# A hybrid decoder trunk on one core: the recurrent branch's gate products as three passes of split operands

## The chip, the core and the metric

The kernel runs on one of the eight cores of a Trainium2 chip. A core has a matrix engine (TensorE, PE in the profile, with its weight loads as PEld), a vector engine (VectorE, DVE), an activation engine (ScalarE, ACT), a general one (GpSimd, POOL), a queue engine that issues most transfers here (SyncE, SP), a work memory (SBUF) and the memory that products accumulate in (PSUM). The engines run side by side, each takes its own instructions in the order written, and semaphores tie them together. The metric is the time of one execution on the device in microseconds (us); times compared are medians of several runs.

## What is computed

Two layers over 256 positions of 2048 channels, all in float32. Each layer normalizes x, projects it (`w_in`), and feeds three branches: a convolution module, a recurrent branch (Griffin's RG-LRU), and sparse attention. Each branch has an output product; the three are weighted by gates, added and projected (`w_o`). Then a squared-ReLU MLP of 8192 channels. The part that the change touches is the two gate products of the recurrent branch, in 6 blocks of 128 channels:

```python
def rg_lru(x, wa, ba, wx, bx, lam):
    b, s, d = x.shape
    xb = x.reshape(b, s, RNN_BLOCKS, RNN_BLOCK_W)
    r = jax.nn.sigmoid((jnp.einsum('bsnc,ncd->bsnd', xb, wa).reshape(b, s, d) + ba).astype(jnp.float32))
    i = jax.nn.sigmoid((jnp.einsum('bsnc,ncd->bsnd', xb, wx).reshape(b, s, d) + bx).astype(jnp.float32))
    log_a = -RG_C * jax.nn.softplus(-lam.astype(jnp.float32)) * r
    a = jnp.exp(log_a)
    gated_x = jnp.sqrt(-jnp.expm1(2.0 * log_a)) * (i * x.astype(jnp.float32))
    _, h = lax.associative_scan(_lin_combine, (a, gated_x), axis=1)
    return h.astype(x.dtype)
...
        r = causal_depthwise_conv(r_x, rnn_conv_w[l], rnn_conv_b[l])
        r = rg_lru(r, rglru_wa[l], rglru_ba[l], rglru_wx[l], rglru_bx[l], rglru_lambda[l])
        p_b = (r * jax.nn.gelu(r_gate)) @ w_rnn_out[l]
```

## The kernel before

**Big products.** All weights stream through SBUF once, as tiles of 128x1024 (`raw`; 768 or 512 wide for the branches' output weights), issued by SP, with four buffers (`wpool`). Each tile is split in two: ACT copies it to `wh`, in the float32r format, and DVE subtracts, `wl = raw - wh`. What is multiplied is split likewise by `split` (`xhl`, `ua`, `rb`, `oh`, `yhl`, `ah`: first half the rounded value, second half the remainder). `tile2` then multiplies 128x128 weights in two passes: `wh` against both halves side by side (512 columns of a PSUM bank `pu`), and `wl` against the first half (256 columns). `unit2` runs 16 such pairs (two weight tiles; 4 or 6 pairs for branch outputs) and makes one unit: 128 output channels by 256 positions. `wnext` keeps three weight tiles ahead. There are four `pu` banks. A unit's bank is emptied by an ACT copy `z<-pu` and a DVE addition `z<-pu,z` (in the MLP's down and the output projection by two DVE additions to x); then it is free for the fourth unit after.

**Side work.** The three branches' small steps are generators (`conv_task`, `rnn_task`, `attn_task`) in a list `side`. `pump`, called between units and weight tiles, advances them while the planner's clocks `clk` for DVE and ACT lie behind PE's; `mm`, `act` and `tt` add an assumed cost to these clocks. So the traced order mixes side steps into the units. After that a scheduler orders each engine's instructions by its own estimate of when they are ready; `keep` pins an instruction behind the one traced before it on its engine..

**The recurrent branch.** `rnn_task` goes through its 6 blocks ("heads" here) in each layer. For head m, GpSimd issues the transfer of the two gate weights (`ruw`, 128x256); DVE makes the short convolution (`rconv`, 4 steps); PE multiplies the two weights by it in float32, 256 columns each, into a side bank `pv`; ACT makes `tr`, `ti` and `t` from it (tanh, tanh, tanh) and an exponential; DVE, ACT (square root) and DVE again prepare the scan; the scan's result times the gate `gg` is split (`rb`) for the branch's output product. ACT changes its function table between some of these (ACT_TABLE_LOAD). It runs once in each layer beside the units of the gates `ga`, of the convolution's output (`pa`, operand `ua`) and of the compression for attention (`wh,cst`).

Lines of the helpers: L134 `tt`, L138 `stt`, L153 `act`, L157 `mm`; L331 the GpSimd addition `ssq` of the norms; L420 the transfer `ruw`.

Of the kernel before, what the change touches and what calls it, by code (L numbers as in the profile page):

```python
# [10 lines left out]
F32R = mybir.dt.float32r  # L11
BF16 = mybir.dt.bfloat16
AF = mybir.ActivationFunctionType
ALU = mybir.AluOpType
# [4 lines left out]
S = 256  # L19
# [74 lines left out]
def trunk(ctx: ExitStack, tc: tile.TileContext, a, out):  # L94
    nc = tc.nc
    V, A, G, T = nc.vector, nc.scalar, nc.gpsimd, nc.tensor
# [10 lines left out]
    keep = tc.keep_in_program_order  # L107
    clk = dict(pe=0.0, v=0.0, act=0.0)

    def hl(dt=F32, name="hl"):  # L110
        return hlp.tile([128, 2, S], dt, tag="hl", name=name)

    def tmp(name="t"):
        return tp.tile([128, S], F32, tag="t", name=name)
# [4 lines left out]
    def big_ps():  # L119
        return psu.tile([128, 512], F32, tag="u", name="pu")  # L120

    def side_ps():
        return pss.tile([128, 512], F32, tag="s", name="pv")

    def fsz(ap):
        n = 1
        for s in ap.shape[1:]:
            n *= s
        return n


    def tt(o, x, y, op):
        clk["v"] += 0.07 + fsz(o) / 960
        return V.tensor_tensor(o, x, y, op=op)  # L134

    def stt(o, x, s, y, op0, op1):
        clk["v"] += 0.07 + fsz(o) / 960
        return V.scalar_tensor_tensor(o, x, s, y, op0=op0, op1=op1)  # L138

    def ts(o, x, s1, s2, op0, op1=None):  # L140
        clk["v"] += 0.07 + fsz(o) / 1920
        if op1 is None:
            return V.tensor_scalar(o, x, s1, None, op0=op0)
        return V.tensor_scalar(o, x, s1, s2, op0=op0, op1=op1)

    def act(o, x, f, bias=None, scale=1.0, accum=None):
        clk["act"] += 0.2 + fsz(o) / 1200
        kw = {}
        if bias is not None:
            kw["bias"] = bias  # L150
        if accum is not None:
            kw["accum_out"] = accum
        return A.activation(o, x, f, scale=scale, **kw)  # L153

    def mm(o, l, r, start, stop, passes=1):
        clk["pe"] += (passes * max(64, fsz(r)) if passes > 1 else max(256, fsz(r))) / 2400 + 0.002
        return T.matmul(o, l, r, start=start, stop=stop)  # L157

    def f32(ap):
        return ap.bitcast(F32)  # L160
# [20 lines left out]

    stream, ready = [], []

    def wtiles():
        raw = wpool.tile([128, 1024], F32, tag="raw", name="raw")
# [20 lines left out]
    def split(dst, src, scale=None):  # L208

        if scale is None:  # L210
            act(dst[:, 0, :], src, AF.Copy)
            tt(dst[:, 1, :], src, f32(dst[:, 0, :]), ALU.subtract)
        else:
            act(dst[:, 0, :], src, AF.Copy, scale=scale)
            stt(dst[:, 1, :], src, scale, f32(dst[:, 0, :]), ALU.mult, ALU.subtract)

    def tile2(p, w, i, r, k, n, between=None):
        h, lo = (v[:, i * 128:(i + 1) * 128] for v in w)
        r1 = mm(p, h, r.rearrange("p a s -> p (a s)"), k == 0, False)
        if between:  # L220
            keep(r1)
            between()
        r2 = mm(p[:, :S], lo, r[:, 0, :], False, k == n - 1)
        if between:
            keep(r2)

    def unit2(p, rhs, between=None):

        k, n = 0, len(rhs)
        while k < n:  # L230
            if k:
                pump()
            w = wnext()
            for i in range(min(8, n - k)):
                tile2(p, w, i, rhs[k], k, n, (between or {}).get(k))
                k += 1
# [19 lines left out]
                stream += halves(a["wup"][l, q * KT + m] if k == "up" else a["wdn"][l, q, m])  # L256


    side = []

    def step():
        v0, a0 = clk["v"], clk["act"]
# [107 lines left out]
    def causal_conv(o, u, w, b, k):  # L370

        ts(o, u, w[:, k - 1:k], b, ALU.mult, ALU.add)
        yield
        for d in range(1, k):
            stt(o[:, d:], u[:, :S - d], w[:, k - 1 - d:k - d], o[:, d:], ALU.mult, ALU.add)
            yield
# [38 lines left out]
    def rnn_task(l, rx, gg, rb_out):  # L415
        rw = par[:, l, P_RW:P_RW + 24]
        for m in range(6):
            rc = tmp("rconv")
            ruw = tmp("ruw")
            keep(G.dma_start(ruw, a["rgw"][l, m]))  # L420
            yield from causal_conv(rc, rx[m], rw[:, 4 * m:4 * m + 4], par[:, l, P_RB + m:P_RB + m + 1], 4)
            p = side_ps()
            mm(p[:, :S], ruw[:, :128], rc, True, True, 4)
            mm(p[:, S:], ruw[:, 128:], rc, True, True, 4)
            tr, ti, t2 = tmp("tr"), tmp("ti"), tmp("t2")
            act(tr, p[:, :S], AF.Tanh, bias=hpar[:, l, 132 + m:133 + m], scale=0.5)
            act(ti, p[:, S:], AF.Tanh, bias=hpar[:, l, 138 + m:139 + m], scale=0.5)
            s2, s4 = sp2[:, l, m:m + 1], sp4[:, l, m:m + 1]

            act(t2, tr, AF.Tanh, bias=s2, scale=s2)  # L430
            act(tr, tr, AF.Exp, bias=s4, scale=s4)
            yield
            stt(t2, tr, 1.0, t2, ALU.add, ALU.mult)
            ts(tr, t2, -1.0, 1.0, ALU.mult, ALU.add)
            stt(t2, t2, 2.0, t2, ALU.subtract, ALU.mult)
            act(t2, t2, AF.Sqrt, scale=-0.25)
            yield
            stt(ti, ti, 1.0, rc, ALU.add, ALU.mult)
            tt(ti, ti, t2, ALU.mult)
            h = rc  # L440
            clk["v"] += 0.6
            V.tensor_tensor_scan(h, tr, ti, 0.0, op0=ALU.mult, op1=ALU.add)
            yield
            tt(h, h, gg[m], ALU.mult)
            r = hl(F32R, "rb_")
            split(r, h, 0.5)
            rb_out.append(r)
            yield
# [241 lines left out]
    for i in range(8):  # L690
        nc.sync.dma_start(x[:, 2 * i:2 * i + 2, :], a["xT"][:, 2 * i:2 * i + 2, :])  # L691
        xs += [scaled(k, gain[:, 0, k:k + 1]) for k in (2 * i, 2 * i + 1)]
        u, c = i % 2, i // 2
        if c % 2 == 0:
            wt[u] = wtiles()
        wpart(wt[u], first[u + 2 * (c // 2)], slice(c % 2 * 512, c % 2 * 512 + 512))
        if u:
            for v in range(2):
                for k in range(4 * c, 4 * c + 4):
                    tile2(early[v], wt[v][1:], k % 8, xs[k], k, KT)  # L700
# [6 lines left out]
    for l in range(L):  # L707

        rc, rb = None, None
# [22 lines left out]
        def evict(nm, m, z):  # L732
# [16 lines left out]
            elif nm == "rgate":  # L749
# [5 lines left out]
                if m == 5:  # L755
                    rt = rnn_task(l, rx, gg, rbt)
                    side.append(rt)
# [26 lines left out]
        for ui, (nm, m) in enumerate(PLAN):  # L784
# [7 lines left out]
            if l == 0 and ui < 2:  # L792
                p = early[ui]
            else:
                p = big_ps()
# [22 lines left out]
        for m in range(KT):  # L818
            p = big_ps()
# [214 lines left out]
```

## Time and profile before

| | |
|---|---|
| median of 3 runs | 2848.22 us (2845.17 to 2848.49) |
| profiled execution, its time | 2845.14 us |
| its span in the trace | 2843.4 us |
| PE busy | 2831.4 us (100%), 16420 passes |
| DVE busy | 2094.7 us (74%) |
| ACT busy | 1473.0 us (52%) |
| GpSimd busy | 96.3 us (3%) |
| granted TensorE clock, mean | 0.999 |
| weight transfers (queue 1) | 529 MB, 56% of the DMA engines' time |

The span is what lies between the first and the last instruction of the trace; the execution's own time is 1.7 us longer. Busy time of an engine is a sum over stages. PE's busy time also covers passes that overlap (a pass of 512 columns is recorded with 0.39 us, and the next starts 0.23 us after it), so the distance between starts is a pass's price, and the recorded duration is not. On ACT and DVE an instruction may start about 0.1 us before the one ahead of it ends.

### The profile page before, as it was taken

What the parts mean: (1) busy time and instruction counts of PE and PEld (TensorE: products, weight loads), DVE (VectorE), ACT (ScalarE), POOL (GpSimd) and SP (SyncE); (2) the same over time, 40 slices, a digit from 0 to 9 for tenths busy, and PEclk for the clock granted to TensorE, in tenths of its full rate; (3) what the DMA queues carried; (4) which work ended last, traced back from release to release, by engine and by line L of the source; (5) the groups of instructions that cost most, each with busy time, mean ns of one, the idle gap of its engine ahead of it and who ended that gap; (6) DMA issues with size and microseconds to landing.
All of it is one profiled execution on the core that took longest, in us unless ns stands there. A gap on an engine that the chain in (4) does not pass through costs nothing.

```text
span 2843.4 us, 43117 instructions
## 1 busy us (share of the span) xinstructions
PE 2831.4 (100%) x16420; PEld 2489.8 (88%) x16420; DVE 2094.7 (74%) x3388; ACT 1473.0 (52%) x2253; POOL 96.3 (3%) x100
## 2 busy tenths in 40 slices
PE   9999999999999999999999999999999999999998
PEld 7888888888888888888888888888888888888887
DVE  7988888777676676666779888786777766756655
ACT  6547766555444343444544587565554444434444
POOL 0000000002000000000200000000020000000001
PEclk9999999999999999999999999999999999999999
DMA  7555654555555555555555556555555555555554
GB/s 241 191 188 177 216 179 161 170 193 192 185 192 189 190 191 188 192 190 189 192 186 192 185 187 215 160 165 178 195 186 192 190 189 192 188 190 191 190 191 148
DMA packets 153454, 534.28 MB, mean 188 GB/s; under 512 B 17312, under 2 KB 18208, under 8 KB 153248
## 3 DMA queue, kind: packets, MB, share of 16 engines
q1 hardware_dynamic: 152192, 529.15, 56.3%
q8 instruction: 128, 2.10, 0.3%
q0 software_dynamic: 768, 2.13, 0.3%
q14 instruction: 78, 0.64, 0.1%
q10 hardware_dynamic: 288, 0.26, 0.0%
HBM read 529.37 MB, written 2.10 MB: 187 GB/s over the span
## 4 chain that ended last, share of the span: by engine, by line
PE 99%; DMA 0%; DVE 0%; ACT 0%; issue 0%; SPq 0%; POOLq 0%; DVEq 0%; ACTq 0%
PE pu L157 96%; PE pv L157 3%; DMA raw<-in_win_dram 0%; PE pv L661 0%; DVE fin L134 0%; ACT wh L153 0%; PE pv L618 0%; DVE wl L134 0%; PE pv L527 0%; DVE xhl L138 0%; SPq L691 0%; POOLq L1026 0%; DVE sq L134 0%; DVEq L1026 0%; ACT sq L153 0%
## 5 line engine op out<-in xcount | busy, mean ns | idle before, releaser
L153 ACT ACTIVATE wh<-raw 128x1024 fp32r<-128x1024 f32 (+2 forms) x1036 | 1067.7, 1031 | 1288.2 <-PE pu L157 682.4
L157 PE MATMUL pu<-xhl,wh 128*128 128x512 f32 x4800 | 1677.1, 393 | 1.3 <-DVE xhl L138 0.8
L134 DVE TENSOR_TENSOR wl<-raw,wh 128x1024 fp32r<-128x1024 f32 (+2 forms) x1036 | 1228.9, 1186 | 593.8 <-ACT wh L153 573.0
L157 PE MATMUL pu<-xhl,wl 128*128 128x256 f32 x4800 | 1345.7, 281 | 0.4 <-DVE wl L134 0.4
L157 PEld LDWEIGHTS pu<-xhl,wh 128*128 128x128 f32 x4800 | 898.0, 187 | 199.0 <-ACT wh L153 1.5
L157 PEld LDWEIGHTS pu<-xhl,wl 128*128 128x128 f32 x4800 | 906.7, 189 | 3.5 <-DVE wl L134 1.2
L157 PE MATMUL pu<-ah,wh 128*128 128x512 f32 x2016 | 699.1, 391 | 0.0
L157 PE MATMUL pu<-ah,wl 128*128 128x256 f32 x2016 | 564.5, 280 | 0.0
L157 PEld LDWEIGHTS pu<-ah,wh 128*128 128x128 f32 x2016 | 377.0, 187 | 82.7
L157 PEld LDWEIGHTS pu<-ah,wl 128*128 128x128 f32 x2016 | 381.0, 189 | 0.0
L134 DVE TENSOR_TENSOR x<-x,pu 128x256 f32<-128x256 f32 x316 | 132.7, 420 | 87.9 <-PE pu L157 82.6
L157 PE MATMUL pu<-yhl,wh 128*128 128x512 f32 x512 | 177.5, 393 | 0.0
L157 PE MATMUL pu<-yhl,wl 128*128 128x256 f32 x512 | 141.7, 277 | 0.0
L331 POOL TENSOR_TENSOR ssq<-ssq,sq 128x256 f32<-128x256 f32 x55 | 74.1, 1347 | 1829.2 <-ACT sq L153 1829.2
L157 PEld LDWEIGHTS pu<-yhl,wh 128*128 128x128 f32 x512 | 95.8, 187 | 22.0
L134 DVE TENSOR_TENSOR z<-pu,z 128x256 f32<-128x256 f32 x268 | 111.4, 417 | 0.8 <-ACT z L153 0.8
L138 DVE SCALAR_TENSOR_TENSOR cacc<-u,hpar,cacc 128x255 f32<-128x255 f32 (+14 forms) x240 | 103.4, 462 | 0.0
L153 ACT ACTIVATE z<-pu 128x256 f32<-128x256 f32 x268 | 97.9, 366 | 1.1 <-PE pu L157 1.1
L157 PEld LDWEIGHTS pu<-yhl,wl 128*128 128x128 f32 x512 | 96.2, 188 | 0.2
L157 PE MATMUL pu<-oh,wh 128*128 128x512 f32 x192 | 67.4, 391 | 0.0
L134 DVE TENSOR_TENSOR z<-z,rb 128x256 f32<-128x256 f32 x136 | 57.4, 424 | 4.3
L138 DVE SCALAR_TENSOR_TENSOR s<-z 128x256 f32<-128x256 f32 x128 | 54.1, 424 | 4.3
(298 smaller groups left out, 1705.3 us busy)
## 6 DMA issues: line engine op xcount, KB each, us to landing
raw<-in_win_dram SPq DMA_DIRECT2D x340, 512.0 KB, 3.2
raw<-in_wup_dram SPq DMA_DIRECT2D x256, 512.0 KB, 4.2
raw<-in_wdn_dram SPq DMA_DIRECT2D x256, 512.0 KB, 4.3
raw<-in_wo_dram SPq DMA_DIRECT2D x64, 512.0 KB, 3.7
raw<-in_wro_dram SPq DMA_DIRECT2D x32, 384.0 KB, 3.1
raw<-in_wao_dram SPq DMA_DIRECT2D x32, 384.0 KB, 3.1
raw<-in_wco_dram SPq DMA_DIRECT2D x32, 256.0 KB, 3.3
raw<-in_cw_dram SPq DMA_DIRECT2D x16, 512.0 KB, 4.6
```

Source lines behind the costliest of these rows:

```text
L134: return V.tensor_tensor(o, x, y, op=op)
L138: return V.scalar_tensor_tensor(o, x, s, y, op0=op0, op1=op1)
L153: return A.activation(o, x, f, scale=scale, **kw)
L157: return T.matmul(o, l, r, start=start, stop=stop)
L331: G.tensor_tensor(ssq[0], ssq[0], q, op=ALU.add)
```

## The change

In `rnn_task`, the convolution's result and the gate weights are split in two, as all big operands are: ACT copies each to float32r (`rs`, `rws`), and GpSimd, not DVE, subtracts to make the remainders. The two float32 products of a head become six float32r passes of 256 columns: high by high, high by remainder, remainder by high, for each gate. A `yield` after the split lets other work be traced in between. In `tile2`, both passes of a pair are now pinned in program order whenever no side work is pending (before: only where a norm's steps are put between two passes).

```diff
@@ tile2
-        if between:
+        if between or not side:
             keep(r1)
+        if between:
             between()
         r2 = mm(p[:, :S], lo, r[:, 0, :], False, k == n - 1)
-        if between:
+        if between or not side:
             keep(r2)
@@ rnn_task
             yield from causal_conv(rc, rx[m], rw[:, 4 * m:4 * m + 4], par[:, l, P_RB + m:P_RB + m + 1], 4)
+            rs, rws = hl(F32R, "rs"), hl(F32R, "rws")
+            for dst, src in ((rws, ruw), (rs, rc)):
+                act(dst[:, 0, :], src, AF.Copy)
+                G.tensor_tensor(dst[:, 1, :], src, f32(dst[:, 0, :]), op=ALU.subtract)
+            yield
             p = side_ps()
-            mm(p[:, :S], ruw[:, :128], rc, True, True, 4)
-            mm(p[:, S:], ruw[:, 128:], rc, True, True, 4)
+            for i in range(2):
+                o, (wh, wl) = p[:, i * S:(i + 1) * S], (rws[:, k, i * 128:(i + 1) * 128] for k in range(2))
+                mm(o, wh, rs[:, 0, :], True, False)
+                mm(o, wh, rs[:, 1, :], False, False)
+                mm(o, wl, rs[:, 0, :], False, True)
```

The scheduler makes new orders of all this. Three places, as built. On ACT, fourth head of layer 1; before the change (here `rb` is the split of the head before, `tr<-pv` the first reader of the gate products, `z<-pu` the emptying of a unit's bank, `t_...` the head's tanh):

```order
L153 ACTIVATE wh<-raw 128x512
L153 ACTIVATE z<-pu 128x256
L153 ACTIVATE rb__16692<-rconv 128x256
L153 ACTIVATE gate<-gate 128x256
L153 ACTIVATE tr<-pv,hpar 128x256
L153 ACTIVATE ti<-pv,hpar 128x256
L153 ACTIVATE wh<-raw 128x1024
```

and the same head after it:

```order
L153 ACTIVATE wh<-raw 128x1024 x2
L153 ACTIVATE rb__16782<-rconv 128x256
L153 ACTIVATE rws<-ruw 128x256
L153 ACTIVATE rs<-rconv 128x256
L153 ACT_TABLE_LOAD
L153 ACTIVATE tr<-pv,hpar 128x256
L153 ACTIVATE ti<-pv,hpar 128x256
L153 ACTIVATE t_16880<-tr,sp_97 128x256
L153 ACTIVATE z<-pu 128x256 x4
```

Before, one bank is emptied ahead of `rb` and `tr`; after, two weight copies, `rb` and the two new copies stand in a row, and four banks are emptied behind `tr`, `ti` and `t`.

On PE at the same head, before:

```order
L157 MATMUL pu<-xhl,wh 128x512
L157 MATMUL pu<-xhl,wl 128x256
L157 MATMUL pv<-rconv,ruw 128x256 x2
L157 MATMUL pu<-xhl,wh 128x512
L157 MATMUL pu<-xhl,wl 128x256
```

and after:

```order
L157 MATMUL pu<-xhl,wh 128x512
L157 MATMUL pu<-xhl,wl 128x256
L157 MATMUL pv<-rs,rws 128x256 x6
L157 MATMUL pu<-ua,wh 128x512
L157 MATMUL pu<-ua,wl 128x256
```

The six passes stand together, at the end of a unit of `xhl`; the unit behind them is one of `ua`, in another bank.

On DVE, the first weight tiles after the two units with which the kernel starts (- before, + after):

```order
 L138 SCALAR_TENSOR_TENSOR xhl<-x,gain,xhl 128x256 x2
 L134 TENSOR_TENSOR wl<-raw,wh 128x512
-L134 TENSOR_TENSOR wl<-raw,wh 128x1024
-L134 TENSOR_TENSOR z<-pu,z 128x256 x2
+L134 TENSOR_TENSOR z<-pu,z 128x256
+L134 TENSOR_TENSOR wl<-raw,wh 128x1024
+L134 TENSOR_TENSOR z<-pu,z 128x256
 L134 TENSOR_TENSOR wl<-raw,wh 128x1024 x4
```

The emptying of the first unit's bank has moved ahead of the first weight tile of the third unit.

## Rows read from the trace of the kernel before

**Rows 1.** The page's part 1: busy us, share of the span, instructions

```profile
PE 2831.4 (100%) x16420; PEld 2489.8 (88%) x16420; DVE 2094.7 (74%) x3388; ACT 1473.0 (52%) x2253; POOL 96.3 (3%) x100
```

**Rows 2.** The page's part 4: the chain that ended last, by engine

```profile
PE 99%; DMA 0%; DVE 0%; ACT 0%; issue 0%; SPq 0%; POOLq 0%; DVEq 0%; ACTq 0%
```

**Rows 3.** PE's waits: engine, line <- releaser: us in total, times, longest

```profile
PE pv L157 <- POOL rc L905: 2.1, 1, 2.1
...
PE pv L157 <- DVE sq L134: 0.7, 1, 0.7
```

**Rows 4.** Stretches with the recurrent branch: from:to us, length, each engine's busy time

```profile
200.00:345.00 145.00, 145.00 (x842) 126.15 (x841) 121.30 (x225) 108.83 (x182) 5.72 (x10) 1.00 0.60 196
...
1600.00:1745.00 145.00, 145.00 (x846) 126.54 (x845) 120.25 (x222) 107.87 (x179) 5.50 (x10) 1.00 0.57 191
```

**Rows 5.** PE in time, fourth head of layer 1: start us, us, operation

```profile
1672.63 0.39 PE L157 MATMUL pu<-xhl,wh 128*128 128x512 f32 x1
1672.86 0.28 PE L157 MATMUL pu<-xhl,wl 128*128 128x256 f32 x1
1672.97 1.03 PE L157 MATMUL pv<-rconv,ruw 128*128 128x256 f32 x4
1673.65 0.58 PE L157 MATMUL pu<-xhl,wh 128*128 128x512 f32 x1
```

**Rows 6.** PE in time at the compression's split passes of 256 columns

```profile
301.13 0.28 PE L157 MATMUL pv<-wl,cst 128*68 128x256 f32 x1
301.25 0.28 PE L157 MATMUL pv<-wh,cst 128*68 128x256 f32 x1
```

**Rows 7.** Groups on ACT: operation and shapes, count | busy us, mean ns | idle before

```profile
L153 ACT ACTIVATE wh<-raw 128x1024 fp32r<-128x1024 f32 x932 | 989.0, 1061 | 1229.6 <-PE pu L157 661.3 <-issue 496.1 <-ACT xhl L153 45.8
...
L153 ACT ACTIVATE z<-pu 128x256 f32<-128x256 f32 x268 | 97.9, 366 | 1.1 <-PE pu L157 1.1
...
L153 ACT ACT_TABLE_LOAD x25 | 32.1, 1283 | 1.2 <-PEq L1020 0.7
...
L153 ACT ACTIVATE t<-tr,sp 128x256 f32<-128x256 f32 x12 | 7.2, 597 | 0.0
```

**Rows 8.** ACT in time, fourth head of layer 1

```profile
1672.72 0.36 ACT L153 ACTIVATE z<-pu 128x256 f32<-128x256 f32 x1
1673.16 0.42 ACT L153 ACTIVATE rb__16692<-rconv 128x256 fp32r<-128x256 f32 x1
...
1675.09 0.46 ACT L153 ACTIVATE tr<-pv,hpar 128x256 f32<-128x256 f32 x1
1675.45 0.47 ACT L153 ACTIVATE ti<-pv,hpar 128x256 f32<-128x256 f32 x1
```

**Rows 9.** A group on DVE: the addition that empties a bank

```profile
L134 DVE TENSOR_TENSOR z<-pu,z 128x256 f32<-128x256 f32 x268 | 111.4, 417 | 0.8 <-ACT z L153 0.8
```

**Rows 10.** GpSimd's additions (ns min/median/max), one of them and DVE around it

```profile
L331 POOL TENSOR_TENSOR ssq<-ssq,sq x55: 925/1372/1466, 637.8 to 2824.1; 128x256 f32<-128x256 f32 x55
...
637.77 1.47 POOL L331 TENSOR_TENSOR ssq<-ssq,sq 128x256 f32<-128x256 f32 x1 [132.36 <-ACT sq L153]
...
636.25 0.47 DVE L138 SCALAR_TENSOR_TENSOR xhl<-x,gain,xhl 128x256 fp32r<-128x256 f32 x1
637.42 1.23 DVE L134 TENSOR_TENSOR wl<-raw,wh 128x1024 fp32r<-128x1024 f32 x1 [0.69 <-ACT wh L153]
638.56 0.96 DVE L138 SCALAR_TENSOR_TENSOR xhl<-x,gain,xhl 128x256 fp32r<-128x256 f32 x1
```

**Rows 11.** PE in time at the start, at 20 us and after the sums of squares

```profile
1.46 4.44 PE L683 MATMUL pv<-wz 128*128 128x512 bf16 x12 [1.46 <-DVE wz L680]
...
20.31 0.39 PE L157 MATMUL pu<-xhl,wl 128*128 128x256 f32 x1 [0.16 <-DVE wl L134]
...
41.39 0.37 PE L157 MATMUL pu<-xhl,wl 128*128 128x256 f32 x1
```

**Rows 12.** Stretches at the end; behind POOL's busy time stands the granted clock

```profile
2836.00:2837.00 1.00, 0.15 (x1) 0.16 (x2) 0.38 (x2) 0.18 (x1) 0.61 (x1) 1.00 0.70 246
...
2838.00:2839.00 1.00, 0.00 (x0) 0.00 (x0) 1.00 (x3) 0.00 (x0) 0.00 (x0) 0.50 0.45 156
```

More of the change, by code (lines that the diff above doesn't have):

```diff
@@ L180, in trunk @@
     G.memset(ebase, 2.718281828459045)
-    stream, ready = [], []
+    stream, ready, side = [], [], []
     def wtiles():
@@ L219, in tile2 @@
         r1 = mm(p, h, r.rearrange("p a s -> p (a s)"), k == 0, False)
+        if between or not side:
+            keep(r1)
         if between:
-            keep(r1)
             between()
         r2 = mm(p[:, :S], lo, r[:, 0, :], False, k == n - 1)
-        if between:
+        if between or not side:
             keep(r2)
@@ L256, in trunk @@
                 stream += halves(a["wup"][l, q * KT + m] if k == "up" else a["wdn"][l, q, m])
-    side = []
     def step():
```

## The prediction

> **What bounds the kernel now.** I read the page from the top: the busy table, the chain, then what PE waited for, then the stretches in which the recurrent branch runs, and there single instructions. PE is busy for 2831.4 of 2843.4 us [rows 1], and the chain that ended last is PE for 99% of the span [rows 2]. After the first 8 us, PE's only waits that the profile lists are 0.7 us for the sums of squares at 40 us and 2.1 us at the very end [rows 3], and 0.16 at 20 us [rows 11]. So nothing can be gained by feeding PE better; time goes down by taking passes off PE, and goes up by whatever makes PE wait. The reader should next see how little room stands behind that full PE: in the two stretches of 145 us where the recurrent branch runs, DVE is busy for about 120 us and ACT for 108 us, and PE for all 145 [rows 4]. DVE and ACT take their work strictly in the order written, so in these stretches an instruction that comes late holds up everything behind it, the weight splits and the emptying of the `pu` banks too.
>
> **The change on PE: passes.** A head's two gate products stand today as four records, 0.68 us from the first to the next weight pass, and that pass is 0.19 us longer than usual (0.58 against 0.39): 0.87 us [rows 5]. A split pass of 256 columns that is not the last of a run starts 0.12 us after the one before [rows 6]; six are 0.70 us. That is 0.17 us a head, 12 heads: **-2.0 us**. It lies on the bound engine, so it is a gain in full. Four more waiting instructions on PE cost some 0.09 us each, as the weight pass at 41.39 does, 0.37 us long instead of 0.28 [rows 11]: +0.3.
>
> **The change on ACT, GpSimd and DVE.** A head gets two ACT copies of 0.4 us and two GpSimd subtractions in a row (24 copies, 24 subtractions in all). ACT has the time as a sum. But the products no longer start when the short convolution and the small weight have arrived: they start after ACT has copied both and GpSimd has made both remainders. GpSimd's price is read from the `ssq` additions of the same size: 0.93 to 1.47 us [rows 10]. Of that about 0.6 is work: the one at 637.77 ends at 639.24, 0.59 after the DVE subtraction that ran when it began (637.42 + 1.23). And DVE pays as well: the `xhl` step that takes 0.47 us alone takes 0.96 us beside GpSimd [rows 10]. The bounds for a remainder are thus 0.6 and 1.5 us; I take 0.9, the nearest row being the one with the least DVE work beside it. The Trainium skill, "SBUF — State Buffer", section "Who interferes with whom", says that a DVE instruction with two SBUF inputs and a GpSimd instruction that reads SBUF lock each other out, and whichever comes first keeps the shared port to its end. The trace agrees (0.59 us after, 0.96 for 0.47). By that rule alone, each subtraction costs DVE up to 0.49 us, 24 x 0.49 = 11.8 us if all of it fell on the path; by the trace most of it falls beside a full PE and costs nothing by itself.
>
> **What the new order does with it.** The end is set by where those late products stand in the fixed orders. I laid the changed order out with the trace's durations: every engine takes its rows in order; each starts when the row before it is done and what it reads or overwrites is free, 0.04 us after the releaser; a remainder takes 0.9 us, or ends 0.6 after the DVE subtraction in its way. Done on the kernel before, this puts no wait over 0.1 us on PE between 45 us and the last product, as the trace shows, and its end is 0.15% off the trace. Done on the changed order, PE waits at a dozen places. The fourth head of layer 1 shows all kinds, and can be followed by hand. *Copies:* on ACT now stand wh, wh, rb, rws, rs in a row, and the second wh needs the buffer that PE's last pass ahead of the six reads. So when PE reaches the six, 1.06 us of wh and three copies of 0.41 are still to come; followers on ACT start about 0.10 before the end of the one ahead (0.36 between tr and ti, both 0.46 to 0.47 long) [rows 7, 8]: 1.06 + 3 x 0.41 - 0.3, with the hand-offs **2.1 us** of waiting. *Remainders:* the weight's begins 0.3 us before the last copy ends and meets a DVE subtraction (1.23 us long [rows 10]), 1.2 us; then 0.9 for the other; less the 0.3 and the first pass: **1.6 us**. *Banks:* the unit right behind the six needs a `pu` bank, and on ACT four z<-pu stand behind tr, ti and t. After the sixth pass (0.28): 0.36 + 0.36 + 0.50 + 0.36 on ACT and 0.42 of z on DVE [rows 7 to 9], with the hand-offs: **2.3 us**. Together 6.0 us at one head. Before, z<-pu (1672.72) runs 2.4 us ahead of tr there, so the bank is free long before PE asks for it [rows 8].
>
> The other places, found in the same way, in us of PE waiting. Layer 0: third head 1.2 (remainder) and 2.4 (bank); fourth 0.4 (remainder), then 1.0 and 1.2 for wh and wl that stand behind the copies; 2.0 near 415 us, a bank behind attention's small steps, whose order moved too; 0.4 at the first pass of the output projection. Layer 1: third head 2.8 (the table load of 1.28 us stands between the six and tr), fourth 6.0, fifth 1.6 (wl) and 1.2 (bank), then 0.9 and 0.9, and again 0.4. That is 8.6 + 13.8 = 22.4 us, and each wait costs 0.09 more, as above: +1.2.
>
> *Start.* With the order pinned, z moves ahead of wl on DVE at 19 us: the subtraction starts 0.4 later, ACT's next step too, and PE, which waits 0.16 us there now [rows 11], waits for 1.1; with the sums of squares some 0.7 later: +1.9, between 0 and 2.4. Elsewhere pinning turns nothing but a few pairs around, which costs nothing on PE.
>
> **The sum**, on the profiled execution's own 2845.1 us: -2.0 + 0.3 + 22.4 + 1.2 + 1.9 = +23.8, 2868.9. That execution lies 3.1 us below the median of the three runs (2848.2, from 2845.2 to 2848.5); half of that added, I say **2870 us**. With remainders of 0.6 us the same layout gives 1 us less, with 1.5 us 3 more; so the size of GpSimd's step is not what decides, but its place in the orders.
>
> **The rivals.** *The remainders are ready in time* (not slower). DVE, ACT and GpSimd run ahead of PE enough, as they do now, and only the passes change: 2845.1 - 2.0 + 0.3, up to 2845 with a start that costs 2: 2843 to 2846, at most 0.2% under the median. It decides where a head's copies and remainders end before PE reaches its six passes. For it: today nothing of these stretches holds PE, though DVE and ACT are busy for three quarters of them and more [rows 4]. Against: at the fourth head the copies, whose price is known, come 2.1 us late by themselves. 0.08. *Only part of the waits.* The copies and remainders hold PE, but z and wl have more lead than I give them: 5 to 8 us of waits, 2849 to 2853: 0.08. *The clock falls too.* Near the end PE has a wait of 2 us and little to do after it, and the granted clock is 0.50 in the stretch that begins at 2838, the 1.2 GHz level, while it is 1.00 up to 2837 [rows 12]. Three waits within 7 us at one head are much the same. What it takes to come back is seen at the start, 12 passes in 4.44 us instead of 12 x 0.23 [rows 11]: 1.7 us for each fall. Two to six falls, and the DVE time of the lock with them: 2874 to 2890. The Trainium skill, "TensorE: Matmul & The Clock Gate", section "Part 1", has the array fall to half rate when PE idles and return with activity; the trace agrees (0.50 after the idle end), and that page speaks against waits that follow each other. 0.20. The change not doing what it says isn't a rival: the passes stand in the order as written.
>
> **Chances.** Forecast as laid out, 2856 to 2877: 0.64. Clock as well: 0.20. Part of the waits 0.08, in time 0.08. Faster by over 0.2% (the least that a measurement of this kernel tells from none) would need 2842.5: 0.03. Within 0.2%, up to 2853.9: 0.12. Slower 0.85. The range reaches from 2850, which leaves out the in-time rival, to 2886.
>
> **What would show it.** In the profile after: PE's waits at 230 to 345 us and 1640 to 1770 us, put down to POOL rs, ACT rs, DVE z and wl, about 20 us in all; six passes of 0.12 at each head; `rs` and `rws` subtractions of 0.9 to 1.4 us; the MLP stretches unchanged to 0.1%. I am wrong in the main step if PE waits under 8 us in these stretches; wrong on the start if PE's waits before 45 us are as now; the clock rival shows as a granted clock under 1 in a window around a head.

## The result, and the profile after

The changed kernel takes **2880.61 us** (median, 2878.96 to 2881.62), the kernel before 2847.14 (2845.17 to 2848.49): ratio **1.0123**, 95% interval 1.0111 to 1.0135. It is 33.5 us slower. The forecast was 2870, slower, with a range of 2850 to 2886: the sign and the range hold, the likeliest case was 10.6 us too low. Two of the four runs of the kernel before lie at 2845 to 2846 us and two at 2848; beside the experiments below its median is 2845.0 to 2845.3. The profiled execution of the changed kernel has a span of 2878.3 us, 34.9 more than the one of before.

Parts 1 and 4 of its page (busy time by engine, the chain that ended last), which answer to [rows 1] and [rows 2]:

```profile
PE 2846.1 (99%) x16444; PEld 2498.0 (87%) x16444; DVE 2103.9 (73%) x3388; ACT 1482.4 (52%) x2277; POOL 120.5 (4%) x124
...
PE 96%; issue 2%; DVE 1%; ACT 1%; DMA 1%; POOL 0%; SPq 0%; POOLq 0%; DVEq 0%; ACTq 0%
```

PE's idle time is 2878.3 - 2846.1 = 32.2 us, where it was 12.0: 20.2 us of the 34.9 are waits. The other 14.7 are in PE's busy time, although its passes became cheaper. A wait counts for more from start to start than as idle time, because the pass ahead of it is recorded longer than its price; counted so, as the prediction did, the waits come to 23.7 us (the table and the start, below). What is left of the second part is where the prediction fell short.

What PE waited for (engine, line <- releaser: us in total, times, longest), the view of [rows 3]:

```profile
PE pu L157 <- DVE z L134: 11.6, 6, 2.8
PE pv L157 <- POOL rs L426: 2.5, 2, 1.4
...
PE pv L157 <- DVE wl L134: 2.0, 2, 1.1
PE pv L157 <- ACT rs L153: 2.0, 1, 2.0
PE pu L157 <- DVE wl L134: 1.9, 5, 0.8
...
PE pv L157 <- DVE sq L134: 1.4, 1, 1.4
```

`DVE z`, the banks, has 11.6 us, more than half of the 20.2 that came with the change. GpSimd, the engine that the change gives new work, releases PE late twice, for 2.5 us in all. 24 subtractions took this long (ns min/median/max):

```profile
L426 POOL TENSOR_TENSOR rs<-rconv,rs x12: 732/917/1822, 237.4 to 1747.6; 128x256 fp32r<-128x256 f32 x12
...
L426 POOL TENSOR_TENSOR rws<-ruw,rws x12: 727/885/2229, 235.2 to 1746.7; 128x256 fp32r<-128x256 f32 x12
```

The stretches of [rows 4], an undisturbed one, and four short ones (from:to us, length, busy time of PE, PEld, DVE, ACT, POOL, then the granted clock):

```profile
200.00:345.00 145.00, 140.04 (x811) 122.77 (x810) 119.12 (x213) 106.21 (x183) 19.66 (x22) 0.98 0.55 183
...
720.00:1420.00 700.00, 700.00 (x4041) 617.08 (x4040) 469.61 (x648) 315.02 (x409) 17.25 (x13) 1.00 0.57 190
...
1600.00:1745.00 145.00, 134.03 (x760) 116.77 (x759) 110.76 (x195) 94.54 (x155) 12.33 (x17) 0.96 0.51 167
...
272.00:280.00 8.00, 6.89 (x24) 5.92 (x24) 5.78 (x15) 4.99 (x11) 0.00 (x0) 0.57 0.26 96
419.00:423.00 4.00, 4.00 (x15) 3.39 (x16) 3.92 (x15) 0.69 (x2) 0.42 (x1) 0.57 0.18 69
1695.00:1700.00 5.00, 4.51 (x17) 3.88 (x18) 4.30 (x11) 3.08 (x7) 0.00 (x0) 0.66 0.43 152
1709.00:1717.00 8.00, 5.94 (x21) 5.10 (x22) 6.50 (x17) 6.37 (x14) 0.00 (x0) 0.57 0.07 22
```

The recurrent stretches lose PE time and have a clock below 1; the MLP (720 to 1420) is as before. The last four rows find the low clock: a mean of 0.57 over 8 us, at the levels 0.5 and 1, is 6.9 us at the lower one (1.2 GHz). Together 6.9 + 3.4 + 3.4 + 6.9 = 20.6 us; each spell begins inside or right behind a PE wait of 1.7 us or more. What that costs is seen where the clock comes back, at 422.5 us (PE in time):

```profile
420.83 0.63 PE L157 MATMUL pu<-rb__2968,wh 128*128 128x512 f32 x1
421.26 0.41 PE L157 MATMUL pu<-rb__2968,wl 128*128 128x256 f32 x1
421.47 0.63 PE L157 MATMUL pu<-rb__3345,wh 128*128 128x512 f32 x1
...
422.64 0.39 PE L157 MATMUL pu<-xhl,wh 128*128 128x512 f32 x1
422.88 0.28 PE L157 MATMUL pu<-xhl,wl 128*128 128x256 f32 x1
422.99 0.40 PE L157 MATMUL pu<-xhl,wh 128*128 128x512 f32 x1
```

A pair takes 421.47 - 420.83 = 0.64 us at the low level and 0.35 at the full one. So each us at the low level in which PE works loses 0.46 us: up to 9.4 us for 20.6. PE is idle in some 2.5 us of that time, so I put it at 8 to 9.

Now the place that the prediction did by hand, the fourth head of layer 1. PE, ACT, GpSimd and one step of DVE in time (start, us, engine, line, operation, in brackets the idle time before and what ended it); for before see [rows 5] and [rows 8]:

```profile
1703.96 0.27 PE L157 MATMUL pu<-xhl,wl 128*128 128x256 f32 x1
1706.18 0.38 PE L157 MATMUL pv<-rs,rws 128*128 128x256 f32 x1 [1.95 <-ACT rs L153]
1707.97 0.86 PE L157 MATMUL pv<-rs,rws 128*128 128x256 f32 x5 [1.40 <-POOL rs L426]
1711.06 0.76 PE L157 MATMUL pu<-ua,wh 128*128 128x512 f32 x1 [2.24 <-DVE z L134]
...
1704.16 1.06 ACT L153 ACTIVATE wh<-raw 128x1024 fp32r<-128x1024 f32 x1 [1.71 <-PE pu L157]
1705.12 0.40 ACT L153 ACTIVATE rb__16782<-rconv 128x256 fp32r<-128x256 f32 x1
1705.42 0.40 ACT L153 ACTIVATE rws<-ruw 128x256 fp32r<-128x256 f32 x1
1705.73 0.40 ACT L153 ACTIVATE rs<-rconv 128x256 fp32r<-128x256 f32 x1
...
1708.86 0.47 ACT L153 ACTIVATE tr<-pv,hpar 128x256 f32<-128x256 f32 x1 [1.43 <-PE pv L157]
1709.23 0.47 ACT L153 ACTIVATE ti<-pv,hpar 128x256 f32<-128x256 f32 x1
1709.59 0.60 ACT L153 ACTIVATE t<-tr,sp 128x256 f32<-128x256 f32 x1
1710.08 1.20 ACT L153 ACTIVATE z<-pu 128x256 f32<-128x256 f32 x4
...
1705.91 1.14 POOL L426 TENSOR_TENSOR rws<-ruw,rws 128x256 fp32r<-128x256 f32 x1 [16.82 <-ACT rws L153]
1707.01 0.90 POOL L426 TENSOR_TENSOR rs<-rconv,rs 128x256 fp32r<-128x256 f32 x1
...
1706.39 0.95 DVE L138 SCALAR_TENSOR_TENSOR rb__16782<-rconv,rb__16782 128x256 fp32r<-128x256 f32 x1
```

Read it from the top: ACT's second `wh` waits 1.71 us for PE and begins at 1704.16, when PE's last pass ahead of the six (1703.96) no longer needs the buffer, and `rb`, `rws` and `rs` stand behind it, so the first of the six passes starts at 1706.18. The two remainders end at 1707.9, and the other five passes start then. The four `z<-pu` stand behind `tr`, `ti` and `t`, and the next unit starts at 1711.06. In starts this is 2.1, 1.7 and 2.4 us; laid out were 2.1, 1.6 and 2.3.

### The profile page after: what moved, and what is told of

Its sections match the earlier page's. It is cut to its first block, busy times and chain, and to the rows that moved or that the text cites. A ratio compares the mean times of both kernels' runs of the same rounds, so it can differ in the third digit from the quotient of the medians.

```text
span 2878.3 us, 43257 instructions
## 1 busy us (share of the span) xinstructions
PE 2846.1 (99%) x16444; PEld 2498.0 (87%) x16444; DVE 2103.9 (73%) x3388; ACT 1482.4 (52%) x2277; POOL 120.5 (4%) x124
## 4 chain that ended last, share of the span: by engine, by line
PE 96%; issue 2%; DVE 1%; ACT 1%; DMA 1%; POOL 0%; SPq 0%; POOLq 0%; DVEq 0%; ACTq 0%
PE pu L157 93%; PE pv L157 2%; DVE wl L134 0%; ACT wh L153 0%; DMA ruw<-in_rgw_dram 0%; PE pv L670 0%; DMA raw<-in_win_dram 0%; DVE fin L134 0%; ACT L153 0%; POOL rs L426 0%; PE pv L627 0%; DVE z L134 0%; POOL rws L426 0%; PE pv L536 0%; ACT ti L153 0%
```

## The experiments

The theory: the work that the change adds costs nothing where it stands beside a full PE; what costs is that the gate products now stand behind it in fixed orders, so PE waits at a few heads, and behind those waits the clock falls. The rivals: the pinning in `tile2` is what holds PE; GpSimd's remainders are what is slow; the clock is no cost of its own. All times below are medians beside runs of the kernel before (2845.0 to 2845.3 us) on the same chip.

**One half of the change at a time.** The pinning alone:

```diff
-        if between:
+        if between or not side:
             keep(r1)
```

> Only the pinning of the passes in `tile2`; the gates as before. Theory (the late gate products hold PE, and the clock falls behind the waits): the order as built, laid out with the durations of the trace before, gives waits of PE of 1.0 us at 20 us, 0.7 more at the sums of squares and 0.4 at the first `yhl` pass of each layer, +2.9 us; and if the slower rhythm of the `yhl` passes (0.353 for 0.347 us a pair in the changed kernel) comes from that wait, 1.8 us more in each layer: 2850 to 2854, granted clock not below 1 after the start. Rival (the pinning holds PE where side work is late): the larger part of the 33 us, 2865 or more.

Measured: 2850.84 us, ratio 1.0017 (1.0009 to 1.0026), +5.7. And the split alone, with `tile2` as before:

> Only the gates' split and six passes; `tile2` as before. Theory: the layout of this order gives 21.7 us of PE waits beyond before, at 267 to 281, 414, 1689 to 1719 and 1747 us, and three or four falls of the clock behind them at 2 us or a little more each: 2869 to 2878; the start and the `yhl` passes as in the kernel before. Rival (the pinning): 2845 to 2855.

Measured: 2876.40 us, ratio 1.0112 (1.0099 to 1.0126), +31.2. So the pinning is the small part. In its trace PE waits at the start and at no head, in the split's at the heads (PE's waits: pinning alone, 12 to 60 us; then split alone, the first of the list for 200 to 1800 us):

```profile
PE pv L157 <- DVE sq L134: 1.4, 1, 1.4
PE pu L157 <- DVE wl L134: 0.8, 1, 0.8
```

```profile
PE pu L157 <- DVE z L134: 9.9, 5, 2.8
PE pv L157 <- ACT wh L153: 2.8, 2, 2.0
PE pv L157 <- POOL rs L425: 2.5, 2, 1.4
```

With the pinning alone the clock is low for 3.4 us at 43 to 46 us, behind the two waits at the start; the expectation had no fall there.

**The work without its place.** The changed kernel makes the copies and remainders and does not use them:

```diff
-            for i in range(2):
-                o, (wh, wl) = p[:, i * S:(i + 1) * S], (rws[:, k, i * 128:(i + 1) * 128] for k in range(2))
-                mm(o, wh, rs[:, 0, :], True, False)
-                mm(o, wh, rs[:, 1, :], False, False)
-                mm(o, wl, rs[:, 0, :], False, True)
+            mm(p[:, :S], ruw[:, :128], rc, True, True, 4)
+            mm(p[:, S:], ruw[:, 128:], rc, True, True, 4)
```

> The changed kernel with the copies and the remainders made as there, but the two gate products taken in float32 from the unsplit operands, as before; the copies' and remainders' results are not used. Theory (not the work of the copies and remainders costs, but that the products stand behind it): the layout gives no wait at the heads, +3.3 us over before, all but 0.4 of it the pinning's: within 1 us of the kernel with the pinning alone, 2850 to 2854. Rival (24 copies and 24 GpSimd subtractions take time of ACT and, by the lock with DVE, of DVE, that is on the path): waits at the heads stay, 2860 or more.

Measured: 2851.05 us, ratio 1.0022 (1.0012 to 1.0031), the same as the pinning alone. GpSimd's subtractions are as slow there as in the changed kernel, and PE is full in the stretch:

```profile
L426 POOL TENSOR_TENSOR rws<-ruw,rws x12: 728/886/2534, 236.1 to 1720.6; 128x256 fp32r<-128x256 f32 x12
...
200.00:345.00 145.00, 145.00 (x842) 126.00 (x841) 126.67 (x224) 112.02 (x193) 17.31 (x22) 1.00 0.60 197
```

DVE is busy 5.4 us longer there than before (126.67 for 121.30; it is 121.92 with the pinning alone), most of it beside GpSimd, and none of it reaches PE. All of the 24 copies and 24 subtractions cost nothing measurable until a product waits for them.

**GpSimd.** The changed kernel without the subtractions (the high halves stand in for the remainders), and with the subtractions on DVE:

```diff
             for dst, src in ((rws, ruw), (rs, rc)):
                 act(dst[:, 0, :], src, AF.Copy)
-                G.tensor_tensor(dst[:, 1, :], src, f32(dst[:, 0, :]), op=ALU.subtract)
...
-                mm(o, wh, rs[:, 1, :], False, False)
-                mm(o, wl, rs[:, 0, :], False, True)
+                mm(o, wh, rs[:, 0, :], False, False)
+                mm(o, wh, rs[:, 0, :], False, True)
```

> The changed kernel without the GpSimd subtractions: the six passes read the high halves alone (rs and rws high for the remainders too), so the gates are less exact. Theory (the ACT copies in their fixed order and the banks behind them, GpSimd only a part): the layout keeps 17.5 us of waits over before, at 271 to 282, 415, 1698 to 1715 and 1757 us, with three or four falls of the clock: 2867 to 2876. Rival (GpSimd's remainders are what comes late): nearly all goes, 2848 to 2855.

Measured: 2874.84 us, ratio 1.0102 (1.0088 to 1.0115), +29.7. PE waits for `rs` from ACT and for the banks, as in the changed kernel (the larger of its waits):

```profile
PE pu L157 <- DVE z L134: 8.1, 4, 2.5
PE pv L157 <- ACT rs L153: 3.2, 2, 2.6
...
PE pv L157 <- ACT wh L153: 1.7, 1, 1.7
```

```diff
-                G.tensor_tensor(dst[:, 1, :], src, f32(dst[:, 0, :]), op=ALU.subtract)
+                tt(dst[:, 1, :], src, f32(dst[:, 0, :]), ALU.subtract)
```

> The changed kernel with the remainders made by DVE (with their cost on the planner's clock) instead of GpSimd. Theory (the place, whichever engine subtracts): the layout gives +23.3 over before, fewer waits at the heads (0.6 and 3.1 near 275, 2.3 near 1697 us) and new ones in attention (450, 543 to 554, 1864, 1970 to 1976 us); waits stand less close together, so one to three falls: 2868 to 2878. Rival (GpSimd is what is slow): 2848 to 2858.

Measured: 2878.62 us, ratio 1.0118 (1.0104 to 1.0132), +33.3, just above the expected range: 13.7 us at the low clock in three stretches, fewer waits at the heads and new ones in attention, as laid out (`DVE e`: 4.3 us in three waits). DVE makes a remainder in 0.42 us (ns min/median/max):

```profile
L134 DVE TENSOR_TENSOR rs<-rconv,rs x12: 414/416/419, 236.4 to 1764.1; 128x256 fp32r<-128x256 f32 x12
```

Without any remainders most of the cost is still there, and with an engine that needs 0.4 us for each the total is the same. But the orders are other ones there, with waits in other places, so this second run does not price GpSimd's speed by itself. By the first, GpSimd's part is the 3 to 4 us by which the changed kernel lies above the one without remainders.

**The same work in another place.** A head's products are written behind the convolution and the split of the next head, so that copies and remainders have a head of lead:

```diff
+        def tail(m, ruw, rc, rs, rws):
             p = side_ps()
...
+            held.append((m, ruw, rc, rs, rws))
+            yield
+            if m:
+                yield from tail(*held.pop(0))
+        yield from tail(*held.pop(0))
```

> All of the change's work and its pinning, but `rnn_task` in another order: a head's products and what follows them are written behind the convolution, copies and remainders of the next head, so that the split has a whole head of lead. Theory (the place of the products): the layout keeps 0.7 us at 327, 0.3 at 1738 and 2.0 us at 410 us (a bank behind attention's steps) and the pinning's 2.9, less 2.0 for the passes: +3.8 over before, 0 to 3.6 more for the `yhl` rhythm and at most two falls of the clock: 2848 to 2856. Rival (the work itself: six passes, copies, GpSimd beside DVE): as the changed kernel, 2872 or more.

> As the kernel with a head of lead, and `tile2` as before the change. Theory: the layout gives +1.0 over before (2.0 us at 408 us stay, passes -2.0): 2845 to 2850, no wait over 1 us at the heads. Rival (the work itself): 2868 or more.

Measured: 2854.37 us, ratio 1.0032 (1.0019 to 1.0044), with the pinning, and 2851.06 us, ratio 1.0020 (1.0011 to 1.0029), without it. The first is within its range, the second 1 us above it. The heads' waits are gone but for one (PE's waits of the first kernel, 200 to 345 us; between 1600 and 1800 us it lists none), and its subtractions are as slow as ever:

```profile
PE pu L157 <- ACT wh L153: 0.8, 1, 0.8
...
L460 POOL TENSOR_TENSOR rws<-ruw,rws x12: 726/887/2222, 234.9 to 1706.7; 128x256 fp32r<-128x256 f32 x12
```

All 72 passes, all copies and all remainders are in this kernel, and 24 of the changed kernel's 33 us are not. That is the main proof of the place. What is left over the kernel before, 5.7 us without the pinning, is in its trace mainly the bank at 410 us (1.7 us), 3.4 us at the low clock behind it (1.6), the output projection's rhythm (1.6, last section) and a wait for `wh` at 326 us (0.6). These make 5.5 by themselves, so the 2 us that the passes give back are not seen in the total. In layer 1, which has none of the four, the time between the same two passes (1476 and 1906 us in the kernel before) is as it was (429.84 us for 429.89): waits and restarts of 0.1 to 0.2 us use the gain up. No version beat the kernel before.

**The clock.** The changed kernel with idle passes where PE's long waits stand, and the changed kernel itself beside it:

```diff
+            b4, b5 = {(0, 2): (8, 10), (1, 2): (0, 11), (1, 3): (8, 10)}.get((l, m), (0, 0))
+            if b4:
+                fp = side_ps()
+                for _ in range(b4):
+                    keep(T.matmul(fp, wzc[:, :128], wzc, start=True, stop=True))
             p = side_ps()
```

(and `b5` of the same kind behind the six passes).

> The changed kernel with idle passes on PE (bf16, of a constant tile, 0.21 us each, their result not used) where its long waits stand: 8 in front of and 10 behind the six passes at the third head of layer 0 and the fourth of layer 1, 11 behind those at the third head of layer 1. Theory (the falls of the clock are a cost of their own behind the waits): PE has 2.7 us more to do than it waits less, by the layout, but the falls at 272, 1695 and 1709 us (17.1 of the 20.5 us at 1.2 GHz, in which a pair takes 0.640 instead of 0.347 us: 7.8 us) go: 4 to 6 us below the changed kernel run beside it, time at the low clock under 7 us. Rival (the clock is no cost of its own, only the waits are): 2 to 3 us above the changed kernel.

> The changed kernel itself, beside the one with filled waits: 2880 us, four falls of the clock as in its first profile, if these belong to its order and not to one execution.

Measured: 2875.08 us with the filled waits, ratio 1.0106 (1.0091 to 1.0121), and 2878.47 without, 1.0116 (1.0099 to 1.0133). The 3.4 us between them are less than expected, the time at the low clock is 13.7 us where under 7 was expected, the intervals overlap, and part of them is the start (the filled kernel lacks the changed one's wait at 20 us). So the two totals prove little; the two layers taken apart show more. Stretches of layer 0 and of layer 1, of the filled kernel and then of the changed one:

```profile
200.00:560.00 360.00, 355.39 (x2063) 309.89 (x2063) 284.39 (x546) 234.47 (x442) 20.26 (x27) 0.98 0.50 173
1600.00:1935.00 335.00, 328.51 (x1927) 284.04 (x1926) 268.91 (x514) 216.97 (x404) 17.06 (x26) 1.00 0.51 175
```

```profile
200.00:560.00 360.00, 352.88 (x2072) 309.27 (x2071) 288.31 (x552) 236.91 (x445) 20.55 (x27) 1.00 0.51 175
1600.00:1935.00 335.00, 322.61 (x1868) 280.80 (x1867) 264.60 (x504) 213.50 (x395) 17.34 (x26) 0.98 0.51 173
```

In layer 1 the falls are gone (clock 1.00 for 0.98). PE's listed waits there fall from 12.4 (in the changed kernel's first profile) to 6.4 us, and the 29 idle passes of 0.22 us add 6.3, which is about the same; yet counted between the same two passes of the big products (again those at 1476 and 1906 us in the kernel before), the layer loses 13.6 us against before, where the changed kernel loses 18.9 (17.4 in its first profile). In layer 0 the 18 idle passes did not keep the clock up: the low time there is 13.7 us, behind the waits that were left, and the layer is 2 to 5 us slower than in the changed kernel. Fewer low us, less time; more low us, more time: the fall is a cost of its own, about 4 to 5 us in layer 1. The total of low time in the changed kernel was 20.5 us in both profiles, but in other places (42, 274, 1694, 1708 and 1728 us in the second): the order sets the waits, and where exactly the clock falls behind them differs between executions. This gives a second test, in which little but the clock differs, for PE's waits from the heads on are the same in the two profiles to within 0.4 us. From 188 to 560 us (passes of the kernel before again) the second profile has 6.8 us less at the low clock and is 2.3 us shorter; from 1476 to 1906 us it has 3.4 more and is 1.5 longer.

## The prediction, point by point

**What bounds the kernel.** Right: PE was full and nothing else had room; the loss is PE waiting, or PE working at half its clock, but for 3.4 us in the output projections.

**Passes.** The six passes start 0.12 us apart where nothing holds them, as [rows 6] had it: -2.0 stands for the passes themselves. One thing was not looked at closely: at most heads the first pass stands apart from the other five, which the layout carries anyway.

**GpSimd's price.** Taken as 0.9 us with bounds of 0.6 and 1.5; the medians are 0.89 and 0.92. Both bounds were off: the shortest took 0.73, and the longest 1.82 and 2.23, with two and more DVE instructions beside them. It did not matter, as said. The Trainium skill, "SBUF — State Buffer", section "Who interferes with whom", has a DVE instruction with two SBUF inputs and a GpSimd instruction that reads SBUF contend for one shared pair of ports, which is locked. This trace agrees, with 0.95 us for `rb`'s DVE step, 0.42 us long elsewhere, at the fourth head. Its price by that rule, put at up to 11.8 us, shows as 5.4 and 2.0 us more of DVE time in the two recurrent stretches of the kernel with the unused split, and as nothing on PE.

**The laid-out order.** The main step was right, place by place (us, from start to start, less the usual distance):

| place | laid out | measured |
|---|---|---|
| layer 0, third head: remainder, bank | 1.2, 2.4 | 1.4, 2.6 |
| layer 0, fourth head: all | 2.6 | 1.8 |
| near 415 us | 2.0 | 1.9 |
| output projection, layers 0 and 1 | 0.4, 0.4 | 0.4, 0.4 |
| layer 1, third head: bank | 2.8 | 2.9 |
| layer 1, fourth head: copies, remainders, bank | 2.1, 1.6, 2.3 | 2.1, 1.7, 2.4 |
| layer 1, fifth head: `wl`, bank | 1.6, 1.2 | 1.1, 1.9 |
| layer 1, then | 0.9, 0.9 | 0.9, 1.0 |
| sum | 22.4 | 22.5 |

**Start.** +1.9 was laid out for it; at 188 us the changed kernel is 1.2 behind in its first profile and 2.5 in its second, which has the fall at 42 us.

**What failed: the choice between the forecast and the third rival.** The prediction gave 0.64 to waits without a fall of the clock and 0.20 to waits with falls. Falls came and cost 8 to 9 us, most of what the forecast is short of. The rival's mechanism and its band (2874 to 2890) were right. The evidence was in the prediction itself: a wait of 2 us before a low clock [rows 12], and a layout with waits of 2.4, 2.8 and 2.3 us and three waits within 7 us. The right weight was the larger one. Its price for one fall, 1.7 us, is near 0.46 x 3.4 = 1.6 for the short spells; two spells were twice as long. The Trainium skill, "TensorE: Matmul & The Clock Gate", section "Part 1", says that the array falls to half rate when PE idles, and the trace agrees: all four spells of the first profile follow waits of 1.7 to 2.8 us.

**What was not in the sum at all:** the output projections, 1.7 us longer in each layer of the profiled execution (last section). "MLP unchanged" holds: 4041 passes between 720 and 1420 us, 4042 before.

The sum, made again with what was measured: waits 22.5, their restarts and the passes about -0.5, start 1.2, clock 8 to 9, output projections 3.4: 34.6 to 35.6, for 34.9 in the profile.

## What to carry to other kernels

When products move from operands that are ready to operands that two more engines must make, the price is not the making, which hides beside a full PE, but the lead that is lost in engines that take their work in order: write the products one stage later than the split, and lay the new order out row by row before timing it. Where the layout shows PE waiting as long as here (the falls came with waits of 1.4 to 2.8 us, though not with each of them), price the fall of the clock behind them as the main case, not as a rival. A count of busy time says nothing of either.

## What was not expected of the hardware

The passes of the output projection (`yhl`) run in one of two rhythms, with no wait and at a full clock. Stretches of 50 us within it, before in both layers and then after in both:

```profile
650.00:700.00 50.00, 50.00 (x291) 43.71 (x290) 37.51 (x45) 25.72 (x36) 12.37 (x9) 1.00 0.56 190
2060.00:2110.00 50.00, 50.00 (x290) 43.70 (x290) 37.60 (x46) 25.73 (x36) 12.37 (x9) 1.00 0.58 190
```

```profile
660.00:710.00 50.00, 50.00 (x285) 43.41 (x284) 36.69 (x45) 25.02 (x35) 11.95 (x9) 1.00 0.55 184
2080.00:2130.00 50.00, 50.00 (x285) 43.31 (x284) 36.67 (x46) 25.12 (x35) 11.83 (x9) 1.00 0.55 183
```

285 passes for 290 or 291: 1.7 us over a projection. Of the other kernels' profiles each shows it in one layer or in both: the pinning alone in layer 1, the split alone in layer 0, the unused split in layer 0, the second profile of the changed kernel in layer 0 only. So it needs neither the pinning nor the split; the kernel before has one profile, so that its own order never has it is not shown. My guess in the expectation of the pinning alone, that the 0.4 us wait at the first `yhl` pass starts it, falls as well: that wait stands in both layers there, and one layer is slow. What sets the rhythm stays open.
